# The depthwise convolution's second channel block, moved from TensorE to ScalarE and GpSimd

## The chip, the core and the metric

One core of a Trainium2 chip runs the whole program. The metric is device time in microseconds (us). Five engines work beside each other, each through its own list of instructions in order: TensorE (PE, and PEld for its weight loads), VectorE (DVE), ScalarE (ACT), GpSimd (POOL) and SyncE (SP). They meet only at semaphores, so an instruction that waits holds everything behind it in its own list.

## What is computed

Two layers over 512 positions of width 1024. The first layer's mixer, in which the change lies, runs a gated causal convolution and an RWKV-7 recurrence side by side and projects both together; a feed-forward block, sliding-window attention and a second feed-forward block follow.

```python
def conv_rwkv_mixer(x, ...):
    p = rms_norm(x, norm_g) @ w_in
    c = p[..., :1024] + conv_in_b
    c = c[..., :512] * sigmoid(c[..., 512:])          # the GLU: 512 channels
    c = causal_dwconv(c, conv_dw_w, conv_dw_b)        # 31 taps for each channel
    c = silu(layer_norm(c, conv_ln_g, conv_ln_b))
    ...                                               # r, decay, k, v, a, b from the rest of p
    y = rwkv7_recurrence(r, decay, k, v, -kk, kk * a) # 8 heads of 64, 512 steps
    ...
    return concatenate([c, y], -1) @ w_out
```

The depthwise convolution of one channel is `y[t] = bias + sum over k of w[30-k] * x[t-k]`, with zeros ahead of the first position.

## The kernel before

Everything lies transposed: channels on the 128 partitions, the 512 positions along the free dimension. The dense products are in fp32 made of three products with a coarse and a fine part of each operand (`gemm`, L174); ScalarE rounds each piece of weights to its coarse part (L150), VectorE takes the difference (L151).

The mixer first makes the keys, values and decays of the recurrence, then inverts the small triangular matrices of its chunks: a loop on VectorE (L489, L491), a way through DRAM, and 32x32 products on TensorE (L520, L527) with copies on ScalarE in between (L522, L529). The recurrence is cut into 8 chunks of 64 positions and 2 groups of 4 heads, so it is 16 units, chunk by chunk, group 0 before group 1. One unit is, in this order on TensorE: L543 (writes px), L549, L556 (from px's copy), L562 (from the copy sv) and L570. Between them stand the copy xs of px (L545: VectorE in group 0, ScalarE in group 1), the copy sv into the state's place (L558, ScalarE, behind the product ds, L553, on VectorE) and the new state (L566 or L568, VectorE), which the same group needs in the next chunk. ScalarE also copies each unit's output (L572).

The convolution's 512 channels are four blocks of 128, j = 0 to 3. `glu(j)` makes a block's input from two dense products, a sigmoid on ScalarE and two instructions on VectorE (L467, L468). Block 0 stays in SBUF (`cp0`) and is summed on VectorE: one activation for the first tap (L618), then 30 multiply-and-adds of 128x511 down to 128x482, each into the sum of the one before (L620). Blocks 1 to 3 go through DRAM: GpSimd's queue writes them into the padded array `cpad` (L470) and reads them back in shifted copies `st` (L628, 8 loads for a block); TensorE multiplies them with diagonal pieces of the taps (`dg`, L623), 32 matmuls of 32 columns for each block (L633), and ScalarE adds the bias (L635). The four sums (`accs`, in the tile `lt`) go into a layer norm, whose first step adds them in pairs (`total`: L641 to L643).

The order within each engine is not written out: a scheduler places each instruction by its own estimates of cost when the program is built, so the convolution's matmuls end up between the inversion's and the recurrence's products. Tiles come from rings of buffers; the ring `td` has two, and its users are the sigmoid `sg`, the GLU's output of the blocks that go through DRAM, and later temporary tiles.

Of the kernel before, what the change touches and what calls it, by code (L numbers as in the profile page):

```python
# [11 lines left out]
F32 = mybir.dt.float32  # L12
F32R = mybir.dt.float32r
I32 = mybir.dt.int32
AF = mybir.ActivationFunctionType
ALU = mybir.AluOpType
# [3 lines left out]
P = 128  # L20
T = 512
# [4 lines left out]
CC = CW // P  # L26
CK = 31
# [36 lines left out]
COL, NCOL = {}, 0  # L64
# [4 lines left out]
class Net:  # L69
# [186 lines left out]
    def mixer(self):  # L256
        nc, tc, ap = self.nc, self.tc, self.ap
        V, S, G = nc.vector, nc.scalar, nc.gpsimd
# [5 lines left out]
        with ExitStack() as es:  # L264
            pool = lambda **k: es.enter_context(tc.tile_pool(**k))
            self.banks(es, "m", "s", m=3, s=3, n=2)
            cst = pool(name="mxc", bufs=1)
# [3 lines left out]
            tb_ = lambda n: tr.tile([P, T], F32, tag="tb", name=n, bufs=TB)  # L271
            td_ = lambda n: tr.tile([P, T], F32, tag="td", name=n, bufs=2)
# [187 lines left out]
            def glu(j):  # L460
                pa = self.gemm(win, j, xh, xl, m=1)[0]
                pb = self.gemm(win, CC + j, xh, xl, m=1)[0]
                sg = td_("sg")
                V.tensor_tensor(out=sg, in0=pb, in1=rstd, op=ALU.mult)
                self.fn(out=sg, in_=sg, func=AF.Sigmoid, bias=self.pc("conv_in_b", CC + j))
                c = cp0 if j == 0 else td_("glu")
                V.tensor_tensor(out=c, in0=pa, in1=rstd, op=ALU.mult)  # L467
                V.scalar_tensor_tensor(out=c, in0=c, scalar=self.pc("conv_in_b", j), in1=sg, op0=ALU.add, op1=ALU.mult)  # L468
                if j:
                    G.dma_start(cpad[j * P : (j + 1) * P, CK - 1 : CK - 1 + T], c)  # L470

            for fc in range(4):
# [13 lines left out]
            for s in range(LH - 1):  # L486
# [3 lines left out]
                                in1=tb[:, 0:n, s : s + 1].to_broadcast([P, n, m]), op=ALU.mult)  # L490
# [10 lines left out]

            zp = cst.tile([P, CK - 1], F32, name="zp")
            G.memset(zp, 0.0)
            for j in range(CC):
                G.dma_start(cpad[j * P : (j + 1) * P, 0 : CK - 1], zp)
                G.dma_start(cpad[j * P : (j + 1) * P, CK - 1 + T :], zp[:, 0 : CPAD - T - CK + 1])
            m32 = cst.tile([P, 1, 1, 32], F32, name="m32")
            for s in range(4):
                G.tensor_copy(m32[s * 32 : s * 32 + 32, 0, 0, :], self.ident[s * 32 : s * 32 + 32, s * 32 : s * 32 + 32])
# [63 lines left out]

            self.table("sigmoid_and_others")
            cp0 = ta("glu0")
            for j in range(CC):
                glu(j)
            self.table("natural_log_exp_and_others")
# [38 lines left out]
            accs, sqs = [[lt[:, o, j, :] for j in range(CC)] for o in range(2)]  # L617
            S.activation(out=accs[0], in_=cp0, func=AF.Identity, scale=self.pc("conv_dw0", CK - 1), bias=self.pc("conv_dw_b", 0))  # L618
            for k in range(1, CK):
                V.scalar_tensor_tensor(out=accs[0][:, k:], in0=cp0[:, 0 : T - k], scalar=self.pc("conv_dw0", CK - 1 - k), in1=accs[0][:, k:], op0=ALU.mult, op1=ALU.add)  # L620
            for j in range(1, CC):
                dg = tr.tile([P, 4, 8, 32], F32, tag="ep", name="dg", bufs=2)
                V.tensor_tensor(out=dg, in0=self.pcs("conv_dw", P)[:, 32 * j : 32 * j + 32].rearrange("p (q g o) -> p q g o", q=4, o=1).to_broadcast([P, 4, 8, 32]), in1=m32.to_broadcast([P, 4, 8, 32]), op=ALU.mult)  # L623
                stk = []
                for q in (2 * j, 2 * j + 1):
                    st = tr.tile([P, 2, CST], F32, tag="t4", name="st", bufs=T4)
                    for s in range(4):
                        G.dma_start(st[s * 32 : s * 32 + 32], cpad[q * 64 : q * 64 + 64, s : s + CST].rearrange("(b p) t -> p b t", p=32))  # L628
                    stk += [st[:, 0], st[:, 1]]
                pc = self.pmm()  # L630
                for g in range(8):
                    for b in range(4):
                        nc.tensor.matmul(pc[b * 32 : b * 32 + 32, :], lhsT=dg[:, b, g, :], rhs=stk[b][:, 4 * g : 4 * g + T],  # L633
                                         start=g == 0, stop=g == 7, tile_position=(0, b * 32))
                S.activation(out=accs[j], in_=pc, func=AF.Identity, bias=self.pc("conv_dw_b", j))  # L635
# [22 lines left out]
            for j in range(CC):  # L658
                V.tensor_tensor(out=accs[j], in0=accs[j], in1=rs, op=ALU.mult)
                c = td_("cact")  # L660
# [384 lines left out]
```

## Time and profile before

| | us |
|---|---|
| median of 3 runs (1216.54 to 1217.11) | 1216.67 |
| the profiled execution | 1216.95 |
| its span, first to last instruction | 1215.2 |
| TensorE busy in it | 1194.8 |
| VectorE | 723.4 |
| ScalarE | 554.3 |
| GpSimd | 72.0 |

The span is the time between the first and the last instruction of the profiled execution; its whole time is 1.75 us longer. Busy shares are means over all stages. An fp32 matmul stands as two records in the trace, so 32 matmuls are 64 records of matmuls; the chain of waits counts weight loads and matmuls as it merges them. The granted clock is 1.00 where TensorE runs at 2.4 GHz and 0.50 where it runs at 1.2.

### The profile page before, as it was taken

Reading aid. Unit: us, or ns where it says so; the run is one execution under the profiler, and the core shown is the slowest. Engines: PE = TensorE matmul, PEld = TensorE weight load, DVE = VectorE, ACT = ScalarE, POOL = GpSimd, SP = SyncE. Lnnn points to the kernel's source line nnn. Section 1 sums busy time; section 2 is a strip of 40 time slices with the busy share of each in tenths; the row PEclk is TensorE's granted clock in tenths of the full one; section 3 lists DMA queues with packets and bytes.
Section 4 is the critical chain, followed back from the end, with each engine's and each line's share of the span. In section 5 each row is a group of like instructions: output and inputs, shape, how many; then the busy total and the mean of one; then the engine's idle time right before and its main releaser. Section 6 shows DMA issues by size and latency. Waiting matters only on the chain.

```text
span 1215.2 us, 16956 instructions
## 1 busy us (share of the span) xinstructions
PE 1194.8 (98%) x6419; PEld 940.5 (77%) x6419; DVE 723.4 (60%) x1366; ACT 554.3 (46%) x1035; POOL 72.0 (6%) x209
## 2 busy tenths in 40 slices
PE   6999999999999999999999999999999999999998
PEld 5777866568788888888888866668888888888886
DVE  6787866477766555553333778875555555553332
ACT  6878332374534444342222567764543343442221
POOL 4101031000100000000000031100000000000000
PEclk9999998999999999999999999999999999999999
DMA  6144291023322223233333231112222223233331
GB/s 191 37 130 113 96 221 38 2 88 103 97 92 104 94 97 104 87 104 96 96 96 95 87 95 57 41 36 90 101 90 101 103 89 104 88 103 112 113 113 61
DMA packets 65088, 114.43 MB, mean 94 GB/s; under 512 B 15680, under 2 KB 17936, under 8 KB 65008
## 3 DMA queue, kind: packets, MB, share of 16 engines
q1 hardware_dynamic: 60048, 102.25, 26.3%
q0 software_dynamic: 4816, 10.89, 3.5%
q8 instruction: 50, 0.82, 0.3%
q14 instruction: 30, 0.25, 0.1%
q10 hardware_dynamic: 144, 0.23, 0.1%
HBM read 105.40 MB, written 4.26 MB: 90 GB/s over the span
## 4 chain that ended last, share of the span: by engine, by line
PE 94%; DVE 2%; ACT 2%; DMA 1%; issue 1%; SPq 0%; DVEq 0%
PE mm L174 68%; PE bank L174 11%; PE mm L633 2%; PE bank L931 2%; PE bank L957 1%; PE bank L950 1%; PE ps L411 1%; PE ps L543 1%; DMA xT<-in_xT_dram 1%; PE ps L562 1%; PE ps L556 1%; PE ps L570 0%; PE bank L359 0%; PE ps L549 0%; PE ps L520 0%
## 5 line engine op out<-in xcount | busy, mean ns | idle before, releaser
L151 DVE TENSOR_TENSOR wlo<-wraw,whi 128x512 fp32r<-128x512 f32 x364 | 250.8, 690 | 348.0 <-ACT whi L150 347.4
L150 ACT CAST whi<-wraw 128x512 fp32r<-128x512 f32 x364 | 224.9, 619 | 421.3 <-PE mm L174 378.4
L174 PE MATMUL mm<-xgh,whi 128*128 128x512 f32 x896 | 350.9, 392 | 9.8 <-ACT whi L150 8.3
L174 PE MATMUL mm<-xgh,wlo 128*128 128x512 f32 x896 | 351.0, 392 | 0.2 <-DVE wlo L151 0.2
L174 PE MATMUL mm<-xgl,whi 128*128 128x512 f32 x896 | 350.5, 391 | 0.0
L174 PEld LDWEIGHTS mm<-xgh,whi 128*128 128x128 f32 x896 | 168.6, 188 | 47.0 <-ACT whi L150 10.1
L174 PEld LDWEIGHTS mm<-xgh,wlo 128*128 128x128 f32 x896 | 168.5, 188 | 38.7 <-issue 2.4
L174 PEld LDWEIGHTS mm<-xgl,whi 128*128 128x128 f32 x896 | 168.7, 188 | 35.8 <-issue 1.2
L174 PE MATMUL mm<-hh,whi 128*128 128x512 f32 x352 | 136.9, 389 | 0.0
L174 PE MATMUL mm<-hl,whi 128*128 128x512 f32 x352 | 136.9, 389 | 0.0
L174 PE MATMUL mm<-hh,wlo 128*128 128x512 f32 x352 | 136.9, 389 | 0.0
L174 PEld LDWEIGHTS mm<-hh,wlo 128*128 128x128 f32 x352 | 66.1, 188 | 13.8
L174 PEld LDWEIGHTS mm<-hh,whi 128*128 128x128 f32 x352 | 66.1, 188 | 13.8
L174 PEld LDWEIGHTS mm<-hl,whi 128*128 128x128 f32 x352 | 66.1, 188 | 13.5
L720 DVE SCALAR_TENSOR_TENSOR t<-gp,col,t 128x512 f32<-128x512 f32 x88 | 63.5, 745 | 0.0
L717 ACT ACTIVATE t<-gp,col 128x512 f32<-128x512 f32 x44 | 35.7, 816 | 35.3 <-DVE gp L715 34.7
L183 ACT CAST hh<-t 128x512 fp32r<-128x512 f32 x44 | 27.2, 622 | 36.8 <-DVE t L723 36.5
L715 DVE TENSOR_TENSOR gp<-mm,rstd 128x512 f32<-128x512 f32 x44 | 30.3, 692 | 17.3 <-PE mm L174 17.2
L723 DVE TENSOR_TENSOR t<-t,mm 128x512 f32<-128x512 f32 x44 | 30.1, 687 | 17.0 <-PE mm L174 17.0
L101 ACT ACTIVATE t<-t 128x512 f32<-128x512 f32 x44 | 27.7, 630 | 20.4 <-DVE t L720 20.3
L714 POOL MEMSET gp<- 128x2 f32 x44 | 4.5, 104 | 507.7 <-DVE t L720 451.0
L936 DVE CUSTOM_DVE_ANT_0 pr<-bank,mask,nsnk 128x256 f32<-128x256 f32 (+1 forms) x64 | 31.4, 503 | 1.9 <-PE bank L931 1.9
(328 smaller groups left out, 1433.6 us busy)
## 6 DMA issues: line engine op xcount, KB each, us to landing
wraw<-in_w_up_dram SPq DMA_DIRECT2D x88, 512.0 KB, 3.5
wraw<-in_w_down_dram SPq DMA_DIRECT2D x40, 512.0 KB, 3.5
wraw<-in_w_in_dram SPq DMA_DIRECT2D x22, 512.0 KB, 3.6
wraw<-in_w_qkv_dram SPq DMA_DIRECT2D x12, 512.0 KB, 3.5
wraw<-in_w_out_dram SPq DMA_DIRECT2D x8, 512.0 KB, 3.5
wraw<-in_w_o_dram SPq DMA_DIRECT2D x8, 512.0 KB, 3.5
st<-cpad POOLq DMA_DIRECT2D x24, 135.0 KB, 4.4
xT<-in_xT_dram SPq DMA_DIRECT2D x4, 512.0 KB, 8.2
```

The lines of the kernel that those rows point to most:

```text
L101: ins = self.nc.scalar.activation(**kw)
L150: nc.scalar.copy(hi, src)
L151: nc.vector.tensor_tensor(out=lo, in0=src, in1=hi.bitcast(F32), op=ALU.subtract)
L174: mm = lambda a, b, **kw: self.nc.tensor.matmul(ps, lhsT=a[:, i, k, :], rhs=b[:, kk, :], **kw)
L183: nc.scalar.copy(hi, src)
L633: nc.tensor.matmul(pc[b * 32 : b * 32 + 32, :], lhsT=dg[:, b, g, :], rhs=stk[b][:, 4 * g : 4 * g + T], start=g == 0, stop=g == 7, tile_pos ...
L715: V.tensor_tensor(out=gp[:, 2:], in0=pg[i], in1=rstd, op=ALU.mult)
L717: S.activation(out=t, in_=gp[:, 2:], func=AF.Identity, scale=self.pc("ffn_conv_w", (3 * l + 2) * FC + f), bias=self.pc("ffn_conv_b", l * F ...
L720: V.scalar_tensor_tensor(out=t, in0=gp[:, j : j + T], scalar=self.pc("ffn_conv_w", (3 * l + j) * FC + f), in1=t, op0=ALU.mult, op1=ALU.add)
L723: V.tensor_tensor(out=t, in0=t, in1=pu[i], op=ALU.mult)
L931: nc.tensor.matmul(pscs[e][:, hp, :nk], lhsT=qr[hs, h // 2, bs], rhs=kd[m][hs, k0 : k0 + nk], start=True, stop=True)
L936: V.tensor_tensor_reduce(out=pr_[:, i, :nk], in0=pscs[e][:, hp, :nk], in1=mask[:, 2 * P - nk :], op0=ALU.add, op1=ALU.min, scale=rq[:, b, ...
```

## The change

Block 1 no longer goes through DRAM. Its GLU output stays in a tile of its own (`glu1`, in the ring `tb`), its taps are loaded once, at the start of the program, into `wt1` by four small loads, and its sum is made tap by tap: ScalarE multiplies the shifted block with a column of taps into a temporary tile `cx` of the ring `td`, and GpSimd adds `cx` to the sum. The first tap, with the bias, is one activation straight into the sum. The write to `cpad`, the loads, the diagonal pieces and the matmuls remain for blocks 2 and 3, and the zeros around them are written for these two.

```diff
@@ glu
-                c = cp0 if j == 0 else td_("glu")
+                c = cps[j] if j < 2 else td_("glu")
...
-                if j:
+                if j > 1:
                     G.dma_start(cpad[j * P : (j + 1) * P, CK - 1 : CK - 1 + T], c)
@@ the zeros around the blocks, and the taps
-            for j in range(CC):
+            for j in range(2, CC):
                 G.dma_start(cpad[j * P : (j + 1) * P, 0 : CK - 1], zp)
                 G.dma_start(cpad[j * P : (j + 1) * P, CK - 1 + T :], zp[:, 0 : CPAD - T - CK + 1])
+
+            wt1 = cst.tile([P, 32], F32, name="wt1")
+            for b in range(4):
+                o = COL["conv_dw"] + 8 * (4 + b)
+                G.dma_start(wt1[b * 32 : b * 32 + 32, :].rearrange("p (s g) -> p s g", s=4), ap["cols"][:, o : o + 8].rearrange("(s p) g -> p s g", s=4))
@@ the tiles
             cp0 = ta("glu0")
+            cps = [cp0, tb_("glu1")]
@@ the sums
-            for j in range(1, CC):
+
+            tap = lambda k: wt1[:, (CK - 1 - k) % 4 * 8 + (CK - 1 - k) // 4 :][:, 0:1]
+            S.activation(out=accs[1], in_=cps[1], func=AF.Identity, scale=tap(0), bias=self.pc("conv_dw_b", 1))
+            for k in range(1, CK):
+                cx = td_("cx")
+                S.activation(out=cx[:, k:], in_=cps[1][:, 0 : T - k], func=AF.Identity, scale=tap(k))
+                G.tensor_tensor(out=accs[1][:, k:], in0=accs[1][:, k:], in1=cx[:, k:], op=ALU.add)
+            for j in range(2, CC):
```

Lines behind the change have new numbers in the changed kernel: L522 becomes L527, L545 L550, L558 L563, L572 L577, L628 L641, L633 L646.

ScalarE, from the first tap of block 0 to the copies tg of the inversion, with what each instruction waits for. Before:

```order
L618 ACTIVATE lt<-glu_1916,col 128x512 [waits PE_49]
L101 ACTIVATE sg<-sg,col 128x512 [waits DVE_49,Activation_49]
L91 ACT_TABLE_LOAD
L522 COPY tg<-ps 32x512 [waits DMAHW4_49,PE_49]
L522 COPY tg<-ps 32x512 [waits PE_49]
```

and with the change:

```order
L624 ACTIVATE lt<-glu_1917,col 128x512 [waits PE_49]
L629 ACTIVATE lt<-glu_1918,col,wt_1277 128x512 [waits DMASW7_49,DMASW1_49,DMASW0_49]
L101 ACTIVATE sg<-sg,col 128x512 [waits DVE_49,Activation_49]
L91 ACT_TABLE_LOAD
L632 ACTIVATE cx<-glu_1918,wt_1277 128x511 [waits DVE_49]
L632 ACTIVATE cx<-glu_1918,wt_1277 128x510 [waits DMASW3_49,DMASW1_49]
L632 ACTIVATE cx<-glu_1918,wt_1277 128x509 [waits Pool_49]
L527 COPY tg<-ps 32x512 [waits DMAHW4_49,PE_49]
L527 COPY tg<-ps 32x512 [waits PE_49]
```

Block 1's first tap now stands ahead of block 3's sigmoid, and three products ahead of the two copies. The second product waits for a DMA of GpSimd's queue (DMASW1 is that of the write of block 3), the third for GpSimd's first sum.

GpSimd, from the first write of a block in this stretch. Before, with nothing left out:

```order
L470 DMA cpad<-glu 128x512
L628 DMA st<-cpad 32x2x540 x5
L470 DMA cpad<-glu 128x512
L628 DMA st<-cpad 32x2x540 x6
L470 DMA cpad<-glu 128x512
L628 DMA st<-cpad 32x2x540 x5
L530 MEMSET sv 64x8x64
L628 DMA st<-cpad 32x2x540 x8
```

and with the change, up to the fourth sum (TENSOR_TENSOR into lt is a sum of block 1):

```order
L470 DMA cpad<-glu 128x512
L641 DMA st<-cpad 32x2x540 x5
L470 DMA cpad<-glu 128x512
L641 DMA st<-cpad 32x2x540
L633 TENSOR_TENSOR lt<-lt,cx 128x511
L641 DMA st<-cpad 32x2x540
L633 TENSOR_TENSOR lt<-lt,cx 128x510
L641 DMA st<-cpad 32x2x540
L633 TENSOR_TENSOR lt<-lt,cx 128x509
L641 DMA st<-cpad 32x2x540
L535 MEMSET sv 64x8x64
L633 TENSOR_TENSOR lt<-lt,cx 128x508
```

The first eight loads are block 2's; the last two of them now stand behind the first and the second sum, and block 3's eight behind the third to the tenth.

ScalarE from the copy sv of unit 5 to that of unit 6. Before:

```order
L558 COPY sv<-ps 64x4x64 [waits DVE_49,PE_49]
L572 COPY y<-ps 128x2x64 [waits PE_49]
L558 COPY sv<-ps 64x4x64 [waits DVE_49,PE_49]
L572 COPY y<-ps 128x2x64 [waits PE_49]
L545 COPY xs<-ps 64x256 [waits PE_49,Activation_49]
```

and with the change:

```order
L563 COPY sv<-ps 64x4x64 [waits DVE_49,PE_49]
L632 ACTIVATE cx<-glu_1918,wt_1277 128x494 [waits Pool_49]
L632 ACTIVATE cx<-glu_1918,wt_1277 128x493 [waits Pool_49]
L632 ACTIVATE cx<-glu_1918,wt_1277 128x492 [waits Pool_49]
L577 COPY y<-ps 128x2x64 [waits PE_49]
L632 ACTIVATE cx<-glu_1918,wt_1277 128x491 [waits Pool_49]
L632 ACTIVATE cx<-glu_1918,wt_1277 128x490 [waits Pool_49]
L563 COPY sv<-ps 64x4x64 [waits DVE_49,PE_49]
```

Five products now stand between two copies of the recurrence, and each waits for the GpSimd sum two before it. On TensorE the order has 5 convolution matmuls ahead of unit 0 (34 before) and 59 in units 0 to 8 (62 before): 8, 8, 8, 5, 0, 7, 8, 8 and 7 of them. On VectorE the copy xs of unit 0 stands behind 15 of block 0's 30 instructions (13 before), and the layer norm's sum of blocks 0 and 1 now waits for GpSimd and stands ahead of unit 8's new state.

## Rows read from the trace of the kernel before

**Rows 1.** The page's busy times: engine, us, share of the span, instructions.

```profile
PE 1194.8 (98%) x6419; PEld 940.5 (77%) x6419; DVE 723.4 (60%) x1366; ACT 554.3 (46%) x1035; POOL 72.0 (6%) x209
```

**Rows 2.** The chain that ended last, in order of time: start us, us, what.

```profile
170.86 6.98 PE mm L633 x58
177.84 2.14 PE ps L520 x64
...
188.15 0.59 PE ps L543 x5
...
189.68 1.08 PE ps L556 x8
...
199.25 0.61 PE ps L543 x8
...
204.79 0.61 PE ps L543 x8
...
206.77 0.60 PE ps L556 x8
...
209.36 0.61 PE ps L543 x8
...
233.34 0.61 PE ps L543 x8
...
238.50 0.55 PE ps L543 x7
...
241.88 0.55 PE ps L543 x7
...
259.36 1.12 PE bank L174 x4
```

**Rows 3.** Timeline of ScalarE: start, us, line, operation, idle before and its releaser.

```profile
160.75 0.72 ACT L101 ACTIVATE sg<-sg,col 128x512 f32<-128x512 f32 x1 [0.29 <-DVE sg L464]
...
170.67 0.82 ACT L618 ACTIVATE lt<-glu,col 128x512 f32<-128x512 f32 x1 [2.10 <-PE mm L174]
...
179.00 0.58 ACT L522 COPY tg<-ps 32x512 f32<-32x512 f32 x1 [5.30 <-PE ps L520]
...
211.99 0.37 ACT L558 COPY sv<-ps 64x256 f32<-64x256 f32 x1 [0.29 <-PE ps L556]
...
231.33 0.37 ACT L558 COPY sv<-ps 64x256 f32<-64x256 f32 x1 [1.33 <-PE ps L556]
```

**Rows 4.** Timeline of GpSimd: the write of block 3.

```profile
173.80 0.59 POOL L470 DMA_DIRECT2D cpad<-glu  x1 [3.77 <-DVE glu L468]
```

**Rows 5.** DMA issues: tensors, queue, count, KB each, median us to landing.

```profile
st<-cpad POOLq DMA_DIRECT2D x24, 135.0 KB, 4.4
...
cpad<-glu POOLq DMA_DIRECT2D x3, 256.0 KB, 4.4
```

**Rows 6.** Timeline of VectorE: block 0's chain and unit 0's copy.

```profile
172.10 0.74 DVE L620 SCALAR_TENSOR_TENSOR lt<-glu,col,lt 128x511 f32<-128x511 f32 x1
...
173.42 6.21 DVE L620 SCALAR_TENSOR_TENSOR lt<-glu,col,lt 128x510 f32<-128x510 f32 x8
...
189.15 0.43 DVE L545 COPY xs<-ps 64x256 f32<-64x256 f32 x1
```

**Rows 7.** GpSimd's instructions by line: count, busy us, mean ns.

```profile
L306 POOL MEMSET s<- 128x512 f32 x1 | 0.5, 530 | 0.0
```

**Rows 8.** Timeline at 312 us, both engines; then VectorE's usual sum (page).

```profile
312.28 0.47 POOL L795 TENSOR_SCALAR_AFFINE_SELECT mask<-mask 128x256 f32<-128x256 f32 x1
...
312.42 0.88 DVE L219 TENSOR_TENSOR sq<-sq 128x512 f32<-128x512 f32 x1
...
L151 DVE TENSOR_TENSOR wlo<-wraw,whi 128x512 fp32r<-128x512 f32 x364 | 250.8, 690 | 348.0 <-ACT whi L150 347.4
```

**Rows 9.** TensorE in stretches: us, busy (records), granted clock, DMA share, GB/s.

```profile
188.00:189.00 1.00, 1.00 (x19) 0.64 0.96 277
...
194.00:195.00 1.00, 1.00 (x13) 0.50 0.00 0
```

## Prediction

> **What bounds the kernel now.** I read the busy shares first, then the chain of work that ended last in order of time, then the timeline of each engine in the stretch of the convolution, then the prices of single instructions. TensorE is busy 98% of the span [rows 1], so work taken off TensorE is worth something only where TensorE does not then wait for something else. The chain shows the stage: the last dense product ends at 170.86 us, and the next dense products (the output projection) start at 259.36 [rows 2]. Between them lie the 96 convolution matmuls (192 records, two per fp32 matmul) and the 16 steps of the recurrence, which I call units 0 to 15 (chunk by chunk, head group 0 then 1). What comes before and after is the same in both kernels, so the result is the shift of that 259.36.
>
> The convolution is filler there. 29 of its matmuls stand in one piece (58 records, 6.98 us) ahead of the small inversion products, the rest is laid four by four into the units. A filled unit takes 4.57 us: unit 3 starts at 204.79 and unit 4 at 209.36. A unit with nothing in it is not free: 238.50 to 241.88 is 3.38 us, because TensorE waits there for the copies on VectorE and ScalarE [rows 2].
>
> **What the change removes.** 32 of the 96 matmuls: 64 records at 6.98/58 us are 7.7 us of TensorE. In the order nearly all of it comes out of the piece in front: before, 34 matmuls ran ahead of unit 0 and 62 in the units; now 5 run ahead and 59 in the units. So the units keep their filler (3 less in unit 3, none in unit 4, again 7 or 8 from unit 5), and the gain must come between 170.86 and unit 0. It also removes one 256 KB write, 8 of the 24 loads and a 1.2 us VectorE product.
>
> **What it adds.** On ScalarE 31 activations of 128x512. The nearest rows are one with a column as bias, 0.72 us, and one with columns for both scale and bias, 0.82 [rows 3]; back to back they come about 0.65 apart. On GpSimd 30 sums of 128x512, of which the trace has none. Lower bound: filling a tile of that size, 0.53 us [rows 7]. A select of 128x256 reads and writes 256 elements in 0.47 [rows 8], so 512 with one input are about 0.94, and a second input at most doubles that: 1.9. I take 1.2, near the one-input row with some of the second read and the hand-over to the next sum, which waits for it. The Trainium skill (GPSIMD Engine Reference, 3.1 Elementwise) gives 4497 ns for such a sum of 2048 elements; a quarter of it, as an estimate, is 1.12 us, and by it the total below would be about 1.5 us lower. No run here shows it yet.
>
> **GpSimd and VectorE exclude each other.** At 312.28 a GpSimd select runs for 0.47 us, and the VectorE sum of two tiles that starts inside it takes 0.88 us, where the usual one takes 0.69; it ends about 0.55 us after the select does [rows 8]. So an instruction with two SBUF inputs waits for the whole GpSimd one. The VectorE chain of block 0 (30 such instructions, eight of them in 6.21 us, so about 0.78 apart, [rows 6]) and the 30 GpSimd sums run at the same time and now largely take turns. The Trainium skill (SBUF — State Buffer, Who interferes with whom) says that a VectorE instruction with at most one SBUF input, such as the copies out of PSUM, does not take part. No row here shows such a pair; without that exemption term C would be some 2 us larger.
>
> **Term A: up to the second product of unit 0 (189.68 before).** Three holds take the place of the 7 us.
> - ScalarE. The products' tile has two buffers, and the second product needs the one that block 3's GLU output leaves through a DMA. The added activation of block 1 stands ahead of the sigmoid and delays that DMA from 173.80 [rows 4] to about 174.1; with 4.4 us to land [rows 5] that is 178.5. Behind the waiting product stand, in ScalarE's queue, the third product and the two copies tg. The first copy began at 179.00 before [rows 3]; now at 179.8, and the products that need it start at 180.4 instead of 180.98. The cover in front is replaced by idle time.
> - GpSimd's queue. The last two loads of block 2 now stand behind sums. The second sum cannot start before 179.2; with 1.2 us and a turn of VectorE the last load is issued at 180.8 and lands at 185.2. Three convolution matmuls wait for it with half of the second inversion products behind them. 5.35 us of small products from 180.4 end at 185.8, the three and the rest add 1.8: unit 0 starts at about 187.6, against 188.15.
> - VectorE. Its copy xs of unit 0, at 189.15 before [rows 6], now stands behind 15 of the 30 instructions (13 before). From 172.1: block 3's product and the 15 are 12 us, the weight split 0.7: 185. Six sums that run in that time hold the chain for about 1.0 us each: 191. So the second product starts at about 191.5: +1.9.
> - The granted clock. It was at the lower level from 188 to 195, after ten microseconds of 32x32 products with little else [rows 9]. Without the dense piece this stretch begins at 170.9 and has gaps, so the fall may come about 7 us sooner and cover the inversion products too: unit 0's second product took 1.08 us at the lower level where unit 3's, at 206.77, took 0.60 [rows 2]. Then unit 0's second product comes near 194: +4.3.
> I take +3.0 (0 to +5).
>
> **Term B: from there to unit 4 (19.68 us before).** Two matmuls fewer (0.5 us), and a gap of 0.7 us in unit 2, which took 5.5 us (199.25 to 204.79, [rows 2]) instead of 4.57, goes because block 3's loads are issued sooner: -1.2 (-2 to 0).
>
> **Term C: VectorE in units 0 to 4.** 15 chain instructions (11.7 us), nine copies and updates (about 3.9) and seven GpSimd sums that hold it (7): 22 us in the 18 that TensorE leaves. The state update is needed only two units later and absorbs part, but the product ds stands in the queue behind the chain, and ScalarE's copy sv waits for ds. I take +1.8 (0 to +4).
>
> **Term D: units 4 to 8, paced by GpSimd.** ScalarE has 4, 5, 5 and 3 products between the copies sv of units 4 to 8, each waiting for the sum two before it. These copies were at 211.99 and 231.33 [rows 3]: 19.34 us. Now 15 sums at 1.2, a product, what is left of a sum and some turns of ds: 19.8. Unit 4 without filler gains 0.8 ahead of this, unit 8 0.6 behind it: -0.9. Every 0.1 us in the price of a sum moves it by 1.5 us: at 0.94 TensorE's own 21.7 us for units 4 to 8 bound it, where they took 23.98 before (209.36 to 233.34, [rows 2]): -2.3; at 1.5 it is +3.6, at 1.9 about +9.
>
> The rest stays. From 233.34 on the units have no convolution; the layer norm's first sum waits for the thirtieth GpSimd sum in front of a state update, which has a unit's slack: 0 (0 to +1.5).
>
> **Sum.** +3.0 - 1.2 + 1.8 - 0.9 = +2.7 us. The profiled execution took 1216.95 us (1.75 outside its span); 0.28 of this is above the median of the runs, so 1216.67 + 2.7 = 1219.4.
>
> **Rivals.**
> - Faster: the freed TensorE time reaches the end. For it: every wait listed is at a queue head and could fall differently, and TensorE bounds the stage. Against: the order leaves the filler in the units. Its mechanism is VectorE's chain keeping its pace beside the sums. Then unit 0's second product comes at about 189.2 (-0.4), B -1.2, C 0, D -2.3: -3.9, 1212.8. It decides from a sum of 1.0 us or less, and a hold of under 0.3 us per sum. Chance 0.22.
> - Balance: the holds and the gains cancel, within 0.2% (2.4 us, about what a measurement of this kernel can tell from no change). For it: A without the sooner clock is +1.9, and C may be absorbed, which gives +1.6 or 0: 1216 to 1219. Chance 0.28.
> - GpSimd sets the pace: a sum at 1.5 to 1.9 us. For it: no row of a two-input GpSimd instruction. It gives D +3.6 to +9 and the total 1224 to 1234. Chance 0.13.
> - That the change does not do what it says: the order shows 32 matmuls fewer, so I give this nothing.
>
> The forecast, slower by 0.2 to 0.5%, has 0.37. Slower by over 0.2% is 0.37 + 0.13 = 0.50, within 0.2% 0.28, faster 0.22. The range from 1211.5 to 1227 reaches over the faster case and the lower part of the last one; for the forecast alone it is 1219 to 1223.
>
> **What would show it.** TensorE idle between 170.9 and 180 with ScalarE's second product ending near 179; the last block 2 load issued near 181; VectorE's chain instructions at 0.7 us or 1.5 and more where sums run, and xs of unit 0 near 191; the granted clock low from before 188; products in units 5 to 7 waiting for GpSimd at the length of a sum; the output projection starting near 262. It is wrong if the sums cost under 1.0 us and the chain keeps its pace, or if unit 0 starts well before 187, which would mean that the loads and the GLU's DMA land much sooner than 4.4 us.

## The result, and the profile after

The changed kernel takes 1232.41 us (median of 4 runs, 1229.96 to 1238.49), the kernel before 1216.89 on the same chip: ratio 1.0133, 95% interval 1.0116 to 1.0150, +15.5 us where +2.7 was predicted. The direction was right, the size was not. The profiled execution has a span of 1230.1 us (before 1215.2) at a mean granted clock of 0.985 (before 0.996).

The busy times, to be held against [rows 1]:

```profile
PE 1200.3 (98%) x6355; PEld 945.0 (77%) x6355; DVE 734.1 (60%) x1365; ACT 573.7 (47%) x1065; POOL 105.3 (9%) x230
```

TensorE has 64 records fewer and is busy 5.5 us longer: the same products ran at a lower clock. The chain in order of time (start us, us, what), against [rows 2]:

```profile
168.50 7.32 DMA st<-cpad
...
175.95 1.92 PE mm L646 x4
177.87 3.39 PE ps L525 x61
...
193.10 0.72 PE ps L548 x5
...
196.43 0.65 PE ps L561 x8
...
213.06 0.43 PE ps L548 x5
...
245.32 0.61 PE ps L548 x8
...
273.42 1.20 PE bank L174 x4
```

(L525 and L532 are the inversion's products, L646 the convolution, L548 and L561 a unit's first and second product, L527 the copies tg, L632 the added products, L633 the sums, L626 VectorE's chain.) In us, with the terms of the prediction:

| stretch | before | after | difference | taken |
|---|---|---|---|---|
| A: second product of unit 0 starts | 189.68 | 196.43 | +6.75 | +3.0 |
| B + C: from there to unit 4 | 19.68 | 16.63 | -3.05 | +0.6 |
| D: units 4 to 8 | 23.98 | 32.26 | +8.28 | -0.9 |
| rest, to the output projection | 26.02 | 28.10 | +2.08 | 0 |

The four add to +14.1 of the 14.9 us by which the two spans differ.

The inversion begins at 177.87 as before (177.84) and takes 15.2 us instead of 10.3. TensorE in stretches (length, then busy us and records of PE, PEld, DVE, ACT, POOL; granted clock; DMA) says why:

```profile
170.00:172.00 2.00, 0.67 (x3) 0.20 (x2) 1.30 (x3) 1.52 (x3) 0.00 (x0) 1.00 0.98 211
172.00:174.00 2.00, 0.00 (x0) 0.00 (x0) 2.00 (x3) 1.97 (x3) 0.31 (x1) 0.65 1.08 212
...
176.00:186.00 10.00, 10.00 (x165) 8.34 (x166) 9.65 (x11) 5.07 (x8) 4.13 (x6) 0.50 0.34 99
186.00:196.00 10.00, 10.00 (x130) 6.79 (x127) 5.97 (x6) 3.65 (x7) 5.71 (x7) 0.50 0.16 44
...
214.00:216.00 2.00, 0.65 (x8) 0.54 (x8) 1.97 (x3) 0.27 (x2) 1.24 (x1) 1.00 0.00 0
...
218.00:220.00 2.00, 2.00 (x10) 0.34 (x8) 0.37 (x1) 1.56 (x3) 1.79 (x3) 0.50 0.00 0
...
232.00:234.00 2.00, 1.37 (x15) 0.39 (x12) 0.00 (x0) 1.37 (x3) 1.92 (x2) 1.00 0.00 0
...
236.00:244.00 8.00, 8.00 (x40) 3.08 (x39) 2.04 (x3) 2.19 (x5) 3.33 (x3) 0.50 0.01 3
```

Three times TensorE stands still or nearly, and the clock then goes from 2.4 to 1.2 GHz (1.00 to 0.50): after 172, after 216, after 234. Not every standstill ends so: from 272 to 274 TensorE is busy for 0.60 of 2 us, and the clock stays at 1.00. The first time it stayed down while TensorE was busy for 20 us without a pause (176 to 196). Before, it fell once in this stage, at 188 [rows 9], and was at 0.57 in the mean from 188 to 196:

```profile
188.00:196.00 8.00, 7.81 (x67) 4.89 (x64) 5.56 (x9) 1.97 (x5) 2.62 (x5) 0.57 0.53 131
```

The standstill ahead of 216 comes from VectorE: the product ds of unit 4 took 1.41 us (214.23 to 215.64) beside a sum, where it takes 0.42 before, and ScalarE's copy sv waited 1.75 us for it.

In units 5 to 8 the other half is seen: ScalarE's timeline (start, us, what, idle before and its releaser), then GpSimd's:

```profile
226.40 0.70 ACT L632 ACTIVATE cx<-glu,wt 128x490 f32<-128x490 f32 x1 [0.67 <-POOL lt L633]
227.01 0.35 ACT L563 COPY sv<-ps 64x256 f32<-64x256 f32 x1
...
233.01 0.70 ACT L632 ACTIVATE cx<-glu,wt 128x485 f32<-128x485 f32 x1 [0.61 <-POOL lt L633]
233.73 0.37 ACT L563 COPY sv<-ps 64x256 f32<-64x256 f32 x1
...
240.51 0.37 ACT L563 COPY sv<-ps 64x256 f32<-64x256 f32 x1 [2.93 <-PE ps L561]
```

```profile
222.44 17.04 POOL L633 TENSOR_TENSOR lt<-lt,cx 128x494 f32<-128x494 f32 x13 [0.26 <-ACT cx L632]
```

Nearly every product waits for a sum, the copy sv waits in line behind five products, and a unit takes about five sums of 1.31 us (17.04/13). VectorE's groups, 170 to 245 us (busy, mean ns), have both the chain and ds, which read two inputs from SBUF, stretched from 732 and 415 ns before. The copy xs out of PSUM takes 428 ns in both kernels:

```profile
L626 DVE SCALAR_TENSOR_TENSOR lt<-glu,col,lt 128x511 f32<-128x511 f32 (+29 forms) x30 | 29.1, 969 | 0.8
L558 DVE TENSOR_TENSOR ds<-sv,dl 64x256 f32<-64x256 f32 x7 | 6.0, 855 | 0.2
```

### The profile page after: what moved, and what is told of

It reads as the page before. It is cut to its first block, busy times and chain, and to the rows that moved or that the text cites. A ratio compares the mean times of both kernels' runs of the same rounds, so it can differ in the third digit from the quotient of the medians.

```text
span 1230.1 us, 16892 instructions
## 1 busy us (share of the span) xinstructions
PE 1200.3 (98%) x6355; PEld 945.0 (77%) x6355; DVE 734.1 (60%) x1365; ACT 573.7 (47%) x1065; POOL 105.3 (9%) x230
## 4 chain that ended last, share of the span: by engine, by line
PE 91%; DVE 3%; ACT 2%; DMA 1%; issue 1%; POOL 1%; DVEq 0%; ACTq 0%; POOLq 0%
PE mm L174 67%; PE bank L174 10%; PE bank L944 2%; PE bank L970 1%; PE mm L646 1%; PE bank L963 1%; PE ps L411 1%; POOL lt L633 1%; PE ps L548 1%; PE ps L567 1%; DMA st<-cpad 1%; PE ps L561 1%; PE ps L525 1%; PE ps L532 1%; DVE lt L626 0%
## 5 line engine op out<-in xcount | busy, mean ns | idle before, releaser
L633 POOL TENSOR_TENSOR lt<-lt,cx 128x511 f32<-128x511 f32 (+29 forms) x30 | 38.0, 1266 | 17.4 <-ACT cx L632 16.0
L101 ACT ACTIVATE t<-t 128x512 f32<-128x512 f32 x44 | 27.7, 630 | 20.4 <-DVE t L733 20.3
```

The lines of the kernel that those rows point to most:

```text
L101: ins = self.nc.scalar.activation(**kw)
L633: G.tensor_tensor(out=accs[1][:, k:], in0=accs[1][:, k:], in1=cx[:, k:], op=ALU.add)
```

## The experiments

Ratios are to the kernel before, run on the same chip, with their 95% interval. "The change" is the changed kernel. The letters are the first letters of the versions' names. Eleven of the eighteen totals (d, e, g, h, i, j, l, n, t, u and w) came out above every range that was expected of them, so what is read from those is their stages.

### Clock and sums, each taken away

Without the products and sums of 30 taps of block 1 (a):

```diff
-            for k in range(1, CK):
-                cx = td_("cx")
-                S.activation(out=cx[:, k:], in_=cps[1][:, 0 : T - k], func=AF.Identity, scale=tap(k))
-                G.tensor_tensor(out=accs[1][:, k:], in0=accs[1][:, k:], in1=cx[:, k:], op=ALU.add)
```

> Leaves out 30 of the 31 taps of block 1: the 30 ScalarE products and 30 GpSimd sums are gone, all else is as in the changed kernel. Clock theory (TensorE without block 1's ready matmuls stands still before the inversion and again in units 5 to 7, and its clock falls): the gap at 170 to 176 us and the fall behind it stay, so unit 0's second product still ends near 195 us, at 5 to 7 us later than before; only what the later falls cost goes; total 1218 to 1224 us. Pace theory (the sums at 1.31 us and ScalarE held by them make units 5 to 8 late): the +8.3 us of units 4 to 8 goes and the sums were most of the loss, total 1212 to 1217 us, at or below the kernel before. Lock theory (GpSimd's sums stretch VectorE's chain and its blocks' work): VectorE's chain instructions come back to 0.74 us each, 1214 to 1220 us.

1222.41 us, ratio 1.0054 (1.0032 to 1.0076): the clock theory's number. No engine has more instructions here than in the kernel before, 32 matmuls are gone, and the kernel is slower than before. A convolution matmul of block 2 waits for its loads at the head of TensorE's queue, in front of the inversion, and unit 0's second product starts at 196.0:

```profile
174.55 1.92 PE L642 MATMUL mm<-st,dg 128*32 128x512 f32 x4 [3.86 <-DMA st<-cpad]
176.40 3.46 PE L525 MATMUL ps<-tg,sv 32*32 32x32 f32 x61
```

This trace is of a run of 1219.43 us at a mean clock of 0.991. Three others took 1229.3 to 1229.8 at 0.981 to 0.982; where these lost more, no trace shows.

The change with block 1's 32 matmuls put back, their result unused (b; the scheduler lays 29 of them ahead of the inversion):

```diff
...
+            pf = self.pmm()
+            for g in range(8):
+                for b in range(4):
+                    nc.tensor.matmul(pf[b * 32 : b * 32 + 32, :], lhsT=df[:, b, g, :], rhs=cps[1], start=g == 0, stop=g == 7, tile_position=(0, b * 32))
```

> The changed kernel with block 1's 32 matmuls of the old shape put back on TensorE (their result is used by nobody); ScalarE's products and GpSimd's sums stay. Clock theory: 29 ready matmuls stand ahead of the inversion again, the granted clock stays at its upper level to about 188 us as in the kernel before, unit 0's second product comes near 190 to 192 us, total 1222 to 1228 us: more work on TensorE makes the kernel faster by 4 to 10 us. Pace and lock theories: TensorE has 7 us more to do, nothing is taken from GpSimd or VectorE, total 1232 to 1238 us.

1224.70 us, ratio 1.0055 (1.0040 to 1.0070): 7.7 us faster than the change by added work. The inversion begins at 177.26, 0.5 us ahead of the change (177.80), so what the matmuls bring at the start is the clock: it is 1.00 from 170 to 280 us and unit 0's second product starts at 190.5. The same two stretches as in the change, and a third:

```profile
176.00:186.00 10.00, 10.00 (x230) 7.09 (x222) 9.72 (x11) 5.80 (x10) 4.86 (x7) 1.00 0.28 93
186.00:196.00 10.00, 10.00 (x139) 5.54 (x137) 9.76 (x10) 5.25 (x10) 6.90 (x9) 1.00 0.21 58
...
222.00:224.00 2.00, 0.43 (x4) 0.00 (x0) 0.00 (x0) 1.40 (x3) 1.92 (x2) 1.00 0.00 0
```

From 222 to 224 TensorE is busy for 0.43 of 2 us and the clock does not fall; why the falls after 216 and 234 are gone too was not followed. Units 4 to 8 still take 29.45 us (208.17 to 237.62), at the upper clock; there 18 sums stand in one piece at 1.35 us:

```profile
209.31 24.33 POOL L639 TENSOR_TENSOR lt<-lt,cx 128x499 f32<-128x499 f32 x18 [1.12 <-ACT cx L638]
```

Both edits together, unused matmuls and no products and sums (p):

> The 32 unused matmuls that hold the clock, and 30 of block 1's 31 taps left out (no products, no sums): the fourth corner beside the changed kernel (1232.4 us), the same without products and sums (1222.4) and with unused matmuls (1224.7). If clock and sums add, 1222.4 - 7.7 = 1214.7 us: the sums cost 10 us with the clock held too. If the sums cost time mostly by making TensorE wait and its clock fall, holding the clock leaves little for them to cost: 1219 to 1223 us. Time bound of GpSimd and lock: VectorE's chain instructions at 0.73 us, units 0 to 8 in 39 us as without sums, 1212 to 1217 us.

1215.34 us, ratio 0.9986 (0.9969 to 1.0004). The four corners as ratios:

| | as it is | clock held by unused matmuls |
|---|---|---|
| with products and sums | 1.0133 | 1.0055 |
| without | 1.0054 | 0.9986 |

Holding the clock is worth 0.7 to 0.8% (8 to 9.5 us) with or without sums, leaving out the sums 0.7 to 0.8% with or without the falls. Within the intervals the two add, and with both taken away no loss is left. Of the clock's part the traces show 5.9 us (with sums) and 3.9 us (without) by unit 0's second product; the rest lies in later falls. The ten runs of this kernel show the clock once more: 1214.7 to 1217.0 us at a mean granted clock of 0.999 to 1.000, and one run of 1223.5 at 0.991, where it fell between 240 and 250 us.

### What the sums cost, and where

Eight buffers for the products, in a tile that is free by then; in the change (d), and in the kernel with unused matmuls (g):

```diff
...
-                cx = td_("cx")
+                cx = cxs[:, k % DC, :]
```

> The changed kernel with ScalarE's products in 8 buffers of their own instead of the ring of 2 that they share with the GLU outputs. Pace theory: ScalarE is no longer held by GpSimd, its copies and scalings for units 5 to 8 come on time, and the +8.3 us of units 4 to 8 shrinks to 0 to 4; total 1224 to 1228 us. Start-hold theory: the 4.2 us for the DMA of block 3 goes too, 2 to 3 us more. Clock theory: the gap at 170 to 176 us stays (block 2's loads are not touched), with its fall; only the later falls may go, total 1226 to 1231 us.

1231.70 us, ratio 1.0128 (1.0093 to 1.0164): nothing gained. The hold on ScalarE is gone, and units 5 to 7 take 4.56 to 4.58 us each beside running sums; but the sums now crowd into units 0 to 3, which take 23.9 us instead of 20.0, VectorE's chain goes from 969 to 1076 ns, and the start is as slow as it was. (The trace is of a run of 1240.35 us; its clock is at 0.50 from 254 to 282, behind the units read here.)

> Both edits together: the 32 unused matmuls that keep TensorE at work, and 8 product buffers that free ScalarE from GpSimd. With the unused matmuls alone the time was 1224.7 us at a mean granted clock of 0.999, and 29.4 us went from unit 4's first product to unit 9's, against 24.0 in the kernel before: 5.5 us. Clock and pace theory (those 5.5 us are ScalarE held by the sums): units 4 to 8 come back to 24 us, the clock stays near 0.999, total 1218 to 1221 us. Lock theory (they are VectorE stretched by the sums, whichever way ScalarE goes): 1223 to 1226 us. If the 8 buffers only let ScalarE run ahead and crowd the sums into units 0 to 4: 1224 to 1228 us.

1230.08 us, ratio 1.0107 (1.0083 to 1.0132), 5 us worse than with the two buffers. Units 4 to 8 are back at 24.97 us, as the pace theory said, and the time is lost ahead of them: the chain takes 1208 ns, unit 0's second product starts at 193.2, unit 4 at 213.8 instead of 208.2. The clock fell there too (0.50 from 190 to 194), unused matmuls or not. The ring of two had also kept sums away from the chain.

With the unused matmuls, two fills in place of each sum (l):

```diff
-                G.tensor_tensor(out=accs[1][:, k:], in0=accs[1][:, k:], in1=cx[:, k:], op=ALU.add)
+                G.memset(accs[1], 0.0)
+                G.memset(cx, 0.0)
```

> As with the 32 unused matmuls (1224.7 us), but each of GpSimd's 30 sums is replaced by two fills that read nothing (0.53 us each in the kernel before), so the sums are left out and GpSimd is busy for about as long. Lock theory (GpSimd's two inputs and VectorE's two inputs exclude each other): VectorE's chain comes back from 1.01 to 0.73 us per instruction; the fills themselves go at 1.06 to 1.15 us a pair, 18 of them in units 4 to 8 take 20 us in place of 24; total 1216 to 1221 us. Theory that busy GpSimd alone slows VectorE (any access): chain near 1.0 us again, 1222 to 1226 us. Theory that ScalarE held by GpSimd's pace is all, lock or none: units 4 to 8 still take 28 us, 1222 to 1225 us.

1239.70 us, ratio 1.0191 (1.0160 to 1.0221). The total answers nothing: the scheduler laid block 3's matmuls behind unit 9, and TensorE waits at 266 to 280 us. What can be read is the price beside a busy GpSimd, of VectorE's chain and then of the fills:

```profile
L626 DVE SCALAR_TENSOR_TENSOR lt<-glu,col,lt 128x511 f32<-128x511 f32 (+29 forms) x30 | 21.9, 731 | 0.7
```

```profile
L640 POOL MEMSET cx<- 128x512 f32 x30 | 15.6, 521 | 13.8 <-ACT cx L638 13.7
L639 POOL MEMSET lt<- 128x512 f32 x30 | 15.6, 519 | 0.0
```

Beside a GpSimd that only writes, the chain keeps its 731 ns (732 in the kernel before).

With the unused matmuls, ca, a bank of PSUM, in place of accs[0] in VectorE's chain (n):

```diff
+            ca = self.bank("n", "ca")
...
+            S.copy(accs[0], ca)
```

> As with the 32 unused matmuls (1224.7 us), but VectorE's chain on block 0 keeps its running sum in a PSUM bank instead of SBUF, so each of its instructions reads one input from SBUF (a copy by ScalarE brings the sum back). Lock theory: the chain no longer takes turns with GpSimd's sums, 0.65 to 0.80 us per instruction in place of 1.01; GpSimd's sums no longer have outliers of 1.5 to 1.9 us; total 1217 to 1223 us. Pace theory (ScalarE held in units 4 to 8 by 18 sums): no change there, 1222 to 1225 us. If what excludes GpSimd is any SBUF read of VectorE: chain near 1.0, 1224 to 1227 us.

1240.26 us, ratio 1.0185 (1.0125 to 1.0246). Here too the order changed (the inversion at 193.1 us), so the total answers nothing. But the chain with its sum in PSUM keeps its price beside GpSimd's sums, on VectorE and on GpSimd:

```profile
180.21 4.53 DVE L627 SCALAR_TENSOR_TENSOR ca<-glu,col,ca 128x487 f32<-128x487 f32 x6
```

```profile
181.92 1.27 POOL L641 TENSOR_TENSOR lt<-lt,cx 128x508 f32<-128x508 f32 x1
183.12 0.55 POOL L649 DMA_DIRECT2D st<-cpad  x1
183.69 1.27 POOL L641 TENSOR_TENSOR lt<-lt,cx 128x507 f32<-128x507 f32 x1
```

So what excludes the two engines is two SBUF inputs against a GpSimd that reads. The Trainium skill (SBUF — State Buffer, Who interferes with whom) states this rule; both runs agree with it (731 ns per instruction with fills; 730 for the 14 from 171 us on with the sum in PSUM; 969 in the change).

### What holds the start

Block 3 instead of block 1 taken from TensorE, with two buffers (c) and with eight (e):

```diff
...
-            cps = [cp0, tb_("glu1")]
+            cps = {0: cp0, 3: tb_("glu3")}
...
-            for j in range(2, CC):
+            for j in (1, 2):
```

> Block 3 instead of block 1 is taken from TensorE (same products and sums, same number of matmuls left); blocks 1 and 2 go through DRAM as in the kernel before. Clock theory: block 1's 29 ready matmuls stand ahead of the inversion again, no fall before 188 us, unit 0's second product near 190 us, and the matmuls that are missing are those of units 4 to 8, where the clock may fall instead; total 1219 to 1226 us. Start-hold theory (the product ring waits for the GLU output's DMA, and block 2's loads stand behind the sums): the same direction, 1224 to 1228 us. Pace theory: the sums are as many and as long, total 1230 to 1235 us.

1226.81 us, ratio 1.0080 (1.0062 to 1.0098). Block 1's 29 matmuls are ahead of the inversion again and unit 0's second product starts at 190.0; with as many sums unit 4 starts at 215.2 instead of 209.3, and the clock falls from 210 on, in waits for xs and sv.

> Block 3 instead of block 1 taken from TensorE, and 8 product buffers. Block 3 alone took 1226.8 us: no fall at the start, but 27 us from unit 0 to unit 4's first product (21 before), 28 us from there to unit 9, and falls in both. Pace theory (ScalarE held by the sums makes those waits): both stretches shrink by 3 to 6 us, total 1215 to 1221 us. Lock theory (VectorE's work is stretched, the sums crowd in earlier): 1224 to 1230 us.

1241.32 us, ratio 1.0201 (1.0183 to 1.0218), against every theory's number. The sums keep VectorE at 98% from 190 to 210 us, as they do with two buffers, and unit 4 starts at 211.6 (215.2 in c). Then TensorE waits 7.6 us for one copy sv, and the clock is at 0.50 from 222 to 240. The copy waits for ds, and ds stands on VectorE behind the layer norm's first sum, which waits for GpSimd's last:

```profile
227.76 0.69 DVE L656 TENSOR_TENSOR lm<-lt 128x512 f32<-128x512 f32 x1 [7.07 <-POOL lt L634]
```

This wait is 1.1 us in the change, and 2.4 to 5.0 us in d, g, i, j and u.

The GLUs of blocks 2 and 3 first, with two buffers (i) and with eight (j):

```diff
-            for j in range(CC):
+            for j in (2, 3, 0, 1):
                 glu(j)
```

> The changed kernel with the GLUs of the blocks that go through DRAM first: blocks 2, 3, 0, 1. The loads of block 2 then start some 6 us earlier, and its matmuls stand ready when the last dense product ends (33 ahead of the inversion); the products no longer wait for the DMA of block 3's GLU output. No work is added. Clock theory: no gap at 170 to 176 us, the clock stays up to near 188 us, unit 0's second product near 190 us; most of 7 us back: 1222 to 1227 us (the later falls in units 5 to 8 stay, or grow, since all conv matmuls are used up early). Pace and lock theories: as after, 1230 to 1235 us.

1250.89 us, ratio 1.0281 (1.0265 to 1.0297), the slowest of all, and my expectation wrong by 25 us. The matmuls were there as planned, but ScalarE now had eight products ahead of the inversion's copies, six of them waiting for a sum: 186.6 us instead of 180.2. TensorE stood 5.4 us in the middle of the inversion, and the clock fell there.

> The reordered GLUs and the 8 product buffers together, nothing unused added: the version that should show what the change is worth without its two faults. Clock and pace theory: no fall at the start and no ScalarE held in units 4 to 8, so the 7 us that TensorE has less to do show, or half of them: 1211 to 1219 us. If TensorE without conv matmuls in units 4 to 8 waits so much that its clock falls there: 1220 to 1230 us. Lock theory: 1221 to 1226 us.

1237.49 us, ratio 1.0163 (1.0135 to 1.0191): no gap at the start, then the chain at 1349 ns and the clock at 0.50 to 0.53 from 210 to 240.

The convolution matmuls that wait for loads ordered behind the inversion, cm being such a matmul and inv the inversion's last product (r); then the same with eight buffers (u):

```diff
...
+                        if j > 1 and not g:
+                            self.after(cm, inv)
```

> The changed kernel with the conv matmuls that wait for loads (blocks 2 and 3) ordered behind the inversion; no work added or taken. Order theory: the inversion begins at about 174 us when its own loads are there, TensorE stands still for 3 to 4 us in place of 5.3, unit 0's second product comes at 186 to 190 us in place of 196.4; if the clock holds, total 1221 to 1226 us. If TensorE needs work in that stretch (light matmuls and waits for ScalarE's copies let the clock fall all the same): the inversion takes 15 us at the lower clock, unit 0's second product at 190 to 194 us, total 1227 to 1232 us.

1226.32 us, ratio 1.0075 (1.0060 to 1.0090), 6 us better than the change, but by neither theory's way: the inversion began at 170.6, and its second products waited for ScalarE, whose copies stood behind a product that waited for a DMA. TensorE, then ScalarE:

```profile
179.82 3.46 PE L532 MATMUL ps<-mbt,tg 32*32 32x32 f32 x61 [6.98 <-ACT tg L527]
```

```profile
177.83 1.33 ACT L632 ACTIVATE cx<-glu,wt 128x510 f32<-128x510 f32 x2 [3.15 <-DMA cpad<-glu]
179.19 1.06 ACT L527 COPY tg<-ps 32x512 f32<-32x512 f32 x2
```

> The full change, waiting matmuls behind the inversion, 8 product buffers. With the order alone: 1226.3 us, unit 0's second product at 194.9 us. Order-and-ring theory: the copies come at 174 to 176 us, TensorE stands still for less than 3 us, the clock holds, unit 0's second product at 183 to 186 us; the sums beside VectorE's chain then take back some: total 1214 to 1220 us. If light work alone lets the clock fall: unit 0's second product at 187 to 190 us, 1219 to 1225 us. Lock theory (VectorE is the bound from here on): whatever the inversion gains waits for VectorE, 1222 to 1228 us.

1231.26 us, ratio 1.0109 (1.0094 to 1.0124). The DMA's hold is gone and the copies come at 178.2, one us sooner: seven products that no longer wait stand in front of them. Units 0 to 3 then take 26.5 us (20.4 in r).

```profile
173.81 4.37 ACT L633 ACTIVATE cxs<-glu,wt 128x511 f32<-128x511 f32 x7
178.21 1.06 ACT L527 COPY tg<-ps 32x512 f32<-32x512 f32 x2
```

### Half of the change

Block 1 with its 16 longer delays on TensorE and 15 products and sums: sums late (h), the order of r added (s), the same with early sums (t), and eight buffers (v for late, w for early).

```diff
...
-                for g in range(8):
+                for g in range(8 if j > 1 else 4):
...
+            for k in range(15):
```

> Half of the change: block 1 keeps its DRAM path and its taps for the delays 15 to 30 on TensorE (16 matmuls, which stand ahead of the inversion), and the delays 0 to 14 go to ScalarE and GpSimd as 15 products and 15 sums onto the evicted half; TensorE has 16 matmuls, 4 us, less to do. Clock theory: no gap at 170 us, no fall before 186 us. Pace and lock theory: half the sums, 15 x 1.25 to 1.35 us = 19 to 20 us in all, end by about unit 4, so units 5 to 8 keep 24 us or less. Together 1211 to 1218 us, at or below the kernel before. If any sums beside VectorE's chain cost more than TensorE gains: 1219 to 1224 us.

1229.76 us, ratio 1.0095 (1.0073 to 1.0118). The 16 matmuls cover 170.6 to 174.1, the first quarter of the inversion's products runs at once, and then a matmul that waits for its load stops TensorE and the clock falls:

```profile
174.10 2.21 PE L525 MATMUL ps<-tg,sv 32*32 32x32 f32 x64
180.33 1.89 PE L640 MATMUL mm<-st,dg 128*32 128x512 f32 x2 [4.03 <-DMA st<-cpad]
```

> Half of the change (15 products and sums, 16 matmuls fewer) with the matmuls that wait for loads behind the inversion. In the half without that order the inversion began at 174.1 us, its first products were done at 176.3, and then TensorE stood still 4.0 us for a load, the clock fell, and unit 0's second product came at 196.0 us (1229.8 us). Order theory: the inversion goes on at the upper clock and ends near 183 us, unit 0's second product at 185 to 188 us, 8 to 11 us earlier; total 1219 to 1222 us with the sums late, where they hold ScalarE in units 5 to 8. If the waits for ScalarE's copies inside the inversion are enough for a fall: 1224 to 1229 us.

1227.42 us, ratio 1.0078 (1.0062 to 1.0095): the load's wait became a wait of 4.1 us for the copies, as in r.

> The same with the 15 sums issued early, between the loads of blocks 2 and 3, beside VectorE's chain. Pace theory (sums hold ScalarE in units 5 to 8 in the one with late sums): they are over by unit 4, units 4 to 8 in 21 to 24 us in place of 28.9, total 1213 to 1218 us. Lock theory (beside the chain each sum costs VectorE as much as itself, 15 x 0.4 to 0.9 us = 6 to 13 us in units 0 to 4): 1219 to 1225 us.

1228.36 us, ratio 1.0092 (1.0077 to 1.0107). Units 4 to 8 take 22.1 us, so late sums do cost them 6.7 us (28.9 in h and s); the chain pays with 910 ns, and the start is as late (196.3). At unit 9 this version has made that up (233.9, 233.3 before); it loses its time behind the recurrence, where the output projection starts 8.5 us later than before and TensorE waits for the convolution's layer norm, as it does in w:

```profile
267.78 0.80 PE L174 MATMUL bank<-mc,whi 128*128 128x512 f32 x1 [4.30 <-ACT mc L183]
```

Why the layer norm comes late was not followed.

> The half with late sums, waiting matmuls behind the inversion, 8 product buffers. Without the buffers: 1227.4 us, unit 0's second product at 194.2 us, because the copies stood 4.1 us behind a product. Order-and-ring theory: unit 0's second product at 184 to 187 us, the sums no longer hold ScalarE; total 1212 to 1219 us. If light work alone lets the clock fall: 187 to 191 us and 1219 to 1224 us.

1220.66 us, ratio 1.0026 (1.0016 to 1.0036), the best version that computes everything, and still slower than before. The copies come at 178.2 here too, the clock falls, unit 0's second product starts at 192.3; from there to unit 9 it takes 43.9 us, as before (43.7).

> The half with early sums, the same order, 8 product buffers. Without the buffers: 1228.4 us, unit 0's second product at 196.3 us, units 4 to 8 in 22.1 us. Order-and-ring theory: unit 0's second product at 184 to 188 us, units 4 to 8 as before it, 1214 to 1220 us. Lock theory: VectorE, stretched by 15 sums beside its chain, gives the units back in 2 to 6 us: 1219 to 1224 us.

1234.02 us, ratio 1.0137 (1.0111 to 1.0164): early sums without the ring's hold take VectorE in units 0 to 3, which take 25.9 us.

## Why the prediction was wrong

Two steps failed: the clock in term A, and the number of sums left in term D. Up to unit 4 the forecast came out nearly right, +3.70 where A, B and C make +3.6, but by luck: A was 3.75 us too low and B + C 3.65 too high. What the total missed lies behind unit 4, in term D (9.2 us) and the rest (2.1).

- **Term A is the first step that failed, in its clock.** Its holds were there as worked out: ScalarE's second product at 178.82 behind the DMA, the first copy tg at 180.17 (predicted 179.8), block 2's last load issued at 180.90 (180.8). What the prediction had as one possibility ("the fall may come about 7 us sooner", +4.3, of which it took a part) happened in full: TensorE stood still from 170.7, since two matmuls ahead of the inversion waited until 175.95 for loads that took 7.3 us, not 4.4, and the inversion took 4.9 us longer at the lower clock. The run with unused matmuls shows that this was the clock: the inversion starts 0.5 us sooner, unit 0's second product 5.9 us (190.5). The idle time itself cost nothing, as assumed; what I had not priced in full was the lower clock of what follows it.
- **The copy xs** came at 194.18 instead of 191, but waited for TensorE, not for the chain. VectorE's hold was real (969 ns) and hidden behind the slow inversion.
- **Terms B and C** came out at -3.05 instead of +0.6. In the kernel before, the fall of the clock lies in this stretch (0.57 from 188 to 196); in the change it came sooner and was over at 196. That an earlier fall also ends earlier was in no term. From unit 0's second product to unit 1 TensorE takes 4.5 us before and 2.6 after:

```profile
189.68 1.08 PE L556 MATMUL ps<-xs,mbt 64*64 64x64 f32 x8 [0.19 <-issue]
...
194.22 1.06 PE L543 MATMUL ps<-sv,mt 128*64 128x64 f32 x8
```

```profile
196.36 0.72 PE L561 MATMUL ps<-xs,mbt 64*64 64x64 f32 x8
...
199.00 0.68 PE L548 MATMUL ps<-sv,mt 128*64 128x64 f32 x8
```

Units 1 and 2 give the other 1.1 us. C's +1.8 for VectorE did not appear: up to unit 4 TensorE waits 0.2 us for xs. With the clock held, from unit 0's second product to unit 4 it was 17.7 us, -2.0.
- **Term D is the second step that failed**, by 9.2 us. It paced units 4 to 8 by 15 sums at 1.2 us. There were 17 of them after unit 4's copy sv, at 1.31; with the clock held 18 at 1.35. Sums that the prediction had done by unit 4 were not: GpSimd had waited 16 us for products, which ScalarE issued one by one between its copies, and 4 us more behind the fill of sv, which waited for the inversion. 18 x 1.35 instead of 15 x 1.2 is +6.3, and units 4 to 8 with the clock held took +5.5 instead of -0.9. The other 2.8 us of the +8.3 I put down to the two falls at 216 and 234 (unit 8 took 9.4 us instead of 5.7).
- **The price of a sum** was nearly right: 1.25 us in the median, 1.27 in the mean (1.21 to 1.72), where 1.2 was taken. The Trainium skill's figure (GPSIMD Engine Reference, 3.1 Elementwise), scaled, gave an estimate of 1.12; the trace differs, and goes first.
- **The rival "GpSimd sets the pace"** (0.13) had the right stage for half of the loss, by a wrong price: the pace came from the number of sums left and their hand-over. That its range (to 1234) holds the measured total is luck: its largest term, +9, makes 1229, and no term makes 1234.
- **The rest**, +2.1 us from unit 9 to the projection, was taken as 0 and not followed by a run of its own; its cause stays open.
- No version that computes everything was below the kernel before, and p, which leaves out the sums, is not told apart from it (0.9969 to 1.0004). In the kernel before, the inversion's first copy came at 179.0 and waited for TensorE, which had the 29 matmuls to do first. In r, s, u, v and w TensorE made the inversion's first products sooner (from 170.5 to 174.3), and the copies still came at 178.1 to 180.0: in front of them on ScalarE stood products of the change. So its own products took back the time that the change had freed on TensorE. Whether products held back behind the copies would free it was not tried.

## What to carry to other kernels

Matmuls that lie over a wait may cost nothing and may be what holds the clock, as the 32 unused ones here: before taking matmuls off TensorE, ask what it does in that stretch without them, price what follows at the lower clock, and ask where the fall ends. Work moved to GpSimd through ScalarE paces everything that is queued behind it on ScalarE; count the sums that will be left when the fillers end, at the price of one beside two-input VectorE work. More buffers are no cure by themselves: of seven pairs here, eight buffers gained in two (s to v 0.5%, i to j 1.2%), changed nothing in one and lost 0.3 to 1.2% in four, where the sums moved to where VectorE was busy or VectorE waited for the last of them.

## What was not expected of the hardware

- After a standstill of 5.3 us the clock stayed at 1.2 GHz through 20 us in which TensorE was busy all the time with 32x32 products and a few of 128x512 (176 to 196 in the change). Behind 29 matmuls of 128x512 the same inversion ran at 2.4 GHz throughout.
- 32 matmuls whose result nobody uses made the changed kernel 7.7 us faster (0.8% by the ratios).
- Time follows the mean granted clock from run to run of one kernel: without products and sums 1219.4 to 1223.0 us at 0.988 to 0.991, and 1229.3 to 1229.8 at 0.981 to 0.982.
- Pairs that exclude each other stretch both ways: sums of 1.25 us in the median took up to 1.95 in the run with block 3 (c), chain instructions of 0.73 up to 1.35 in the mean (j).
